# Seven block products for eight in the down-projection, with its sums of y made in the up phase

## The chip, the core and the metric

One core of a Trainium2 chip runs the whole layer in one launch. The time is device time of the launch in microseconds (us). TensorE (PE) multiplies, VectorE (DVE) and ScalarE (ACT) do elementwise work and empty PSUM, GpSimd (POOL) and the SyncE queue (SP) issue the transfers. Each engine takes its instructions in the order in which they stand in its queue; an instruction that waits holds up all that stand behind it on that engine.

## What is computed

The layer is a streaming encoder step over 1072 tokens (16 meta tokens, 1024 prompt frames, 32 sample frames). The part that the change touches is the feed-forward:

```
h = rmsnorm(x, g)
u = h @ w_up                                  # 1024 -> 2 x 2816
gate, up = u[..., :D_FF], u[..., D_FF:]
gate_ext = concatenate([gate_past, gate], axis=1)
y = silu(depthwise_causal_conv(gate_ext, dw_w, dw_b)) * up
return x + y @ w_down                          # 2816 -> 1024
```

All of it is float32. The kernel makes each float32 product from three matmuls: an operand is split into a high half (a rounded copy, made by ACT) and a low half (operand minus high half, made by DVE), and high x high, high x low and low x high are added up in PSUM.

## The kernel before

Features lie on the 128 partitions, tokens along the free axis. The 2816 hidden features are 22 tiles of 128 (f = 0 to 21), the 1024 model features are 8 tiles (k, or m on the output side).

**Up phase.** Tiles 0 and 1 are computed plainly. For tiles 2 to 21 the 2 x 2 block product (gate and up rows by two halves of the model features, times two token blocks) is made with 7 block products for 8 (`up_strassen`). The tokens are two halves p = 0 and p = 1 of two blocks of 266 or 264 tokens each (`PNS`), so a tile takes 7 products x 2 halves x 12 matmuls = 168 matmuls. The products run in the order `SEQ_ = (1, 5, 6, 2, 7, 3, 4)`, p = 0 and p = 1 in turn. Products 1, 6, 7, 4 of one half add into one PSUM bank, 5 and 3 into a second, 2 has a third; after each product the bank is copied out by ACT or added to a row by DVE, and the next product of that bank can only start after that. The moving operands (forms) of the products lie split in memory: 1 to 4 in `BH`/`BL`, 5 to 7 in `THI`/`TLO` (`th`, `tl`). The weights' forms of the next tile (sums of the weight blocks, split) are made by ACT and DVE during the present tile (`w_forms`). When the gate rows are done, `gate_done` runs the convolution and the swish over 1058 tokens, `y_done` multiplies with the up rows and stores y of the tile in DRAM (`yd`). Rows of even tiles (`rows1`) and odd tiles (`rows0`) lie in the memory of X, in `gx0` and in `rbt` (`rb`).

**Down phase.** It runs in three chunks of 8, 8 and 6 tiles (`CHUNKS`). Chunks 0 and 1 take, for each of 8 output tiles, three token blocks of 384, 352 and 320 tokens with 8 x 3 matmuls each (`d_mm`, by lines 238 to 240). Output tile m of chunk 0 is copied into X, chunk 1 adds to it. The residual (`xd`) is added by accumulating transfers that POOL issues after each second output tile of chunk 0. The weights come one output tile ahead (`d_load`). The split y of a chunk lies where the operands of the up phase lay: `y_load` brings a tile of y (528 KB) from DRAM to a staging row and `hilo` splits it (ACT the high half, DVE the low half). Chunk 0 takes four staging rows and `rbt` during tile 21; later tiles use two rows, `gx0` and `rbt`, in turn. The last chunk of 6 tiles is run together with the final norm, in an order written out by hand.

**Order.** TensorE's order is that of the code up to the end of the down phase. The order on the other engines there is set by a scheduler, which also puts SP's and POOL's transfers in a row. In the part that is written by hand at the end DVE and ACT are in the code's order too.

Of the kernel before, what the change touches and what calls it, by code (L numbers as in the profile page):

```python
# [10 lines left out]
F32 = mybir.dt.float32  # L11
# [81 lines left out]
CHUNKS = ((0, 8), (8, 16), (16, 22))  # L93
# [62 lines left out]
def body(nc, tc, cp, wp, xp, dp, io):  # L156
# [920 lines left out]
    yd = dp.tile([NF, P, T], F32, tag="yd", name="yd")  # L1077

# [48 lines left out]
    with tc.tile_pool(name="psB", bufs=1, space=PSUM, reuse_waits="tile") as pf:  # L1127
# [33 lines left out]
        def w_forms(f):  # L1161
            w = ups[f] = Up()
            g, u, s = raws3
            nc.sync.dma_start(g, up_src(f, 0))
            nc.sync.dma_start(u, up_src(f, 1))
# [3 lines left out]
            A, B = slice(0, 512), slice(512, 1024)  # L1169
# [15 lines left out]
            free.extend((hg, lg, h12, l12, a22, h34, l34))  # L1185
# [6 lines left out]
        def moving(q, p, j):  # L1192
            n, a = PNS[p], PAT[p] - H0
            b = a + n
            if q == 1:
                return BH[:, j, a:b], BL[:, j, a:b]
            if q == 2:
                return BH[:, 4 + j, a:b], BL[:, 4 + j, a:b]
            if q == 3:
                return BH[:, 4 + j, b:b + n], BL[:, 4 + j, b:b + n]  # L1200
            if q == 4:
                return BH[:, j, b:b + n], BL[:, j, b:b + n]
            i = {5: 0, 6: 1, 7: 2}[q]
# [66 lines left out]
        def y_done(f):  # L1270
            _, Tm, Y = rows_of(f)
            nc.vector.tensor_tensor(out=Y[:, NMETA:NPR], in0=Y[:, NMETA:NPR], in1=Tm[:, NMETA:NPR], op=ALU.mult)
            nc.vector.tensor_tensor(out=Y[:, NPR:T], in0=Y[:, NPR:T], in1=Tm[:, GS:GOW], op=ALU.mult)
            nc.sync.dma_start(yd[f][:, NMETA:T], Y[:, NMETA:T])

        def evac(f, p, what, ps):
            G, _, Y = rows_of(f)
            n, a0 = PNS[p], PAT[p]
            b0 = a0 + n
            ya, yb = Y[:, a0:a0 + n], Y[:, b0:b0 + n]  # L1280
            ga = G[:, g_at(a0):g_at(a0) + n]
            gb = [(lo_, hi_, G[:, o:o + hi_ - lo_]) for lo_, hi_, o in g_pieces(b0, n)]
            add = nc.vector.tensor_tensor
            if what == 1:
                nc.scalar.copy(ga, ps)
            elif what == 2:
                add(out=ga, in0=ga, in1=ps, op=ALU.add)
            elif what == 5:
                nc.scalar.copy(yb, ps)
            elif what == 6:  # L1290
                for lo_, hi_, z in gb:
                    nc.scalar.copy(z, ps[:, lo_:hi_])
            elif what == 7:
                add(out=yb, in0=yb, in1=ps, op=ALU.add)
            elif what == 3:
                for lo_, hi_, z in gb:
                    add(out=z, in0=z, in1=ps[:, lo_:hi_], op=ALU.add)
            else:
                nc.scalar.copy(ya, ps)

        BANK = {1: 0, 6: 0, 7: 0, 4: 0, 5: 1, 3: 1, 2: 2}
        SEQ_ = (1, 5, 6, 2, 7, 3, 4)
        FIRST = (1, 5, 2)

        def up_strassen(f, steps):
            gate_start(f)
            banks = {}
            for q, p in steps:
                k = p, BANK[q]
                if q in FIRST:  # L1310
                    banks[k] = mmt()[:, :PNS[p]]
                product(banks[k], q, p, f, q in FIRST)
                evac(f, p, q, banks[k])
                if (q, p) == (3, 1) and f < NF - 1:
                    gate_done(f)
                yield
# [33 lines left out]
        for i in range(4):  # L1350
            group(0, 1, i // 2, i % 2)
            if i == 0:
# [6 lines left out]
        for i, (u, p, c) in enumerate(((0, 1, 0), (0, 1, 1), (1, 1, 0), (1, 1, 1), (0, 0, 0), (0, 0, 1), (1, 0, 0), (1, 0, 1))):  # L1359
            group(1, u, p, c)  # L1360
            if i == 3:
# [25 lines left out]
        trow = [trow[i] for i in (0, 3, 1, 4, 2, 5)]  # L1387
        sr = rows(sl, 4)
        yrow = trow + [(sr[0], sr[1]), (sr[2], sr[3])] + list(zip(rows(BH, KD), rows(BL, KD))) + trow
        first = [xf[1][:, 0:ny], xf[1][:, ny:2 * ny], xf[2][:, 0:ny], xf[2][:, ny:2 * ny], rbt[:, 0:ny]]  # L1390
        first += first[:3]
        later = [gx0[:, 0:ny], rbt[:, 0:ny]]

        def y_load(f):
            raw = first[f] if f < CHUNKS[0][1] else later[f % 2]
            nc.sync.dma_start(raw, yd[f][:, NMETA:T])
            hilo(*yrow[f], raw)

        bhf, blf = flat(BH), flat(BL)
        dring = [(plain[3], plain[0]), (plain[2], plain[1])]  # L1400
        slw = [sl[:, i * 1024:i * 1024 + 1024] for i in range(4)]
# [215 lines left out]
```

## Time and profile before

| | us |
|---|---|
| median of 3 runs (1090.02 to 1090.47) | 1090.44 |
| the profiled execution | 1091.2 |
| its span in the trace | 1089.4 |
| TensorE busy | 1062.2 |
| VectorE busy | 777.3 |
| ScalarE busy | 471.9 |
| up phase from tile 2 on | 406.4 to 818.5 |
| chunks 0 and 1 of the down phase | 818.5 to 1004.0 |
| last chunk, final norm, stores | 1004.0 to 1089.4 |

The page of the profile gives the busy time of each engine and its share of the span. A busy TensorE only says that matmuls are in flight; how fast they go is read from how many start in a stretch. The timeline lists instructions with start, duration and, in brackets, the idle time before one and what ended it. An SP row with a q is the issue of a transfer, not its landing.

### The profile page before, as it was taken

What the parts mean: (1) busy time and instruction counts of PE and PEld (TensorE: products, weight loads), DVE (VectorE), ACT (ScalarE), POOL (GpSimd) and SP (SyncE); (2) the same over time, 40 slices, a digit from 0 to 9 for tenths busy, and PEclk for the clock granted to TensorE, in tenths of its full rate; (3) what the DMA queues carried; (4) which work ended last, traced back from release to release, by engine and by line L of the source; (5) the groups of instructions that cost most, each with busy time, mean ns of one, the idle gap of its engine ahead of it and who ended that gap; (6) DMA issues with size and microseconds to landing.
All of it is one profiled execution on the core that took longest, in us unless ns stands there. A gap on an engine that the chain in (4) does not pass through costs nothing.

```text
span 1089.4 us, 18949 instructions
## 1 busy us (share of the span) xinstructions
PE 1062.2 (98%) x7549; PEld 1035.2 (95%) x7549; DVE 777.3 (71%) x1355; ACT 471.9 (43%) x1009; POOL 144.9 (13%) x189
## 2 busy tenths in 40 slices
PE   8999999989999899999999999999999999999996
PEld 7999997758999899999999999999999999999996
DVE  7799999999877788778778778778777203222344
ACT  8532227996766854334334334334354214011321
POOL 1111000012435120000000001001001111000232
PEclk9999999999999999999999999999999999999998
DMA  7344331125853211321221221221267846222013
GB/s 264 81 109 100 83 95 40 39 56 82 161 147 110 66 60 60 101 77 60 99 79 59 99 79 60 97 79 60 79 237 200 193 85 159 58 63 59 15 58 102
DMA packets 48288, 103.77 MB, mean 95 GB/s; under 512 B 10048, under 2 KB 27704, under 8 KB 48200
## 3 DMA queue, kind: packets, MB, share of 16 engines
q1 hardware_dynamic: 38376, 84.46, 23.9%
q0 software_dynamic: 9536, 17.89, 9.9%
q8 instruction: 59, 0.97, 0.4%
q10 hardware_dynamic: 288, 0.22, 0.1%
q14 instruction: 29, 0.24, 0.1%
HBM read 72.41 MB, written 21.02 MB: 86 GB/s over the span
## 4 chain that ended last, share of the span: by engine, by line
PE 63%; DVE 3%; ACT 2%; issue 1%; POOL 0%; POOLq 0%; DVEq 0%; ACTq 0%
PE mm L1211 38%; PE mm L240 8%; PE mm L238 8%; PE mm L239 8%; ACT hraw L1231 1%; DVE tl L1143 1%; ACT bh L273 0%; ACT th L1142 0%; PE R L262 0%; DVE x L1485 0%; POOL rb L270 0%; ACT acc L269 0%; DVE traw L1233 0%; DVE wlo L1143 0%; DVE x L1264 0%
## 5 line engine op out<-in xcount | busy, mean ns | idle before, releaser
L364 DVE SCALAR_TENSOR_TENSOR acc<-glu,prm,acc 128x1090 f32<-128x1090 f32 (+3 forms) x180 | 168.1, 968 | 0.4
L1211 PE MATMUL mm<-bh,sl 128*128 128x266 f32 (+1 forms) x544 | 117.5, 285 | 0.0
L238 PE MATMUL mm<-hi,whi 128*128 128x352 f32 (+3 forms) x312 | 104.8, 336 | 0.0
L239 PE MATMUL mm<-lo,whi 128*128 128x352 f32 (+3 forms) x312 | 102.2, 328 | 1.6 <-DVE lo L274 1.5
L240 PE MATMUL mm<-hi,wlo 128*128 128x352 f32 (+3 forms) x312 | 101.7, 326 | 0.0
L1211 PEld LDWEIGHTS mm<-bh,sl 128*128 128x128 f32 x544 | 90.7, 189 | 0.0
L1211 PE MATMUL mm<-th,sl 128*128 128x264 f32 (+1 forms) x384 | 90.2, 285 | 0.0
L1211 PE MATMUL mm<-bl,sl 128*128 128x266 f32 (+1 forms) x296 | 84.5, 285 | 0.0
L1211 PE MATMUL mm<-bh,whi 128*128 128x266 f32 (+1 forms) x320 | 80.9, 285 | 0.0
L238 PE MATMUL mm<-bh,whi 128*128 128x266 f32 (+4 forms) x224 | 68.2, 304 | 0.0
L240 PE MATMUL mm<-bh,wlo 128*128 128x266 f32 (+4 forms) x224 | 67.9, 303 | 0.1
L239 PE MATMUL mm<-bl,whi 128*128 128x266 f32 (+4 forms) x224 | 67.9, 303 | 0.0
L1211 PEld LDWEIGHTS mm<-th,sl 128*128 128x128 f32 x384 | 66.2, 188 | 0.0
L1211 PE MATMUL mm<-th,wlo 128*128 128x266 f32 (+1 forms) x240 | 65.4, 285 | 0.0
L239 PEld LDWEIGHTS mm<-lo,whi 128*128 128x128 f32 x312 | 59.2, 190 | 3.3 <-DVE lo L274 3.0
L238 PEld LDWEIGHTS mm<-hi,whi 128*128 128x128 f32 x312 | 59.1, 189 | 1.3 <-DVE acc L364 0.6
L240 PEld LDWEIGHTS mm<-hi,wlo 128*128 128x128 f32 x312 | 59.0, 189 | 0.0
L1211 PEld LDWEIGHTS mm<-bh,whi 128*128 128x128 f32 x320 | 57.1, 189 | 0.0
L1211 PEld LDWEIGHTS mm<-bl,sl 128*128 128x128 f32 x296 | 55.8, 188 | 0.0
L1211 PE MATMUL mm<-bh,wlo 128*128 128x266 f32 (+1 forms) x208 | 51.7, 285 | 0.0
L1211 PE MATMUL mm<-th,rawr 128*128 128x266 f32 (+1 forms) x208 | 49.1, 285 | 0.0
L1211 PE MATMUL mm<-bh,rawr 128*128 128x266 f32 (+1 forms) x208 | 49.0, 285 | 0.0
(374 smaller groups left out, 3250.0 us busy)
## 6 DMA issues: line engine op xcount, KB each, us to landing
x<-wup SPq DMA_DIRECT2D x40, 512.0 KB, 4.0
wlo<-raw POOLq DMA_DIRECT2D x16, 512.0 KB, 4.5
raw<-wdn SPq DMA_DIRECT2D x16, 512.0 KB, 6.7
yd<-x SPq DMA_DIRECT2D x12, 528.0 KB, 2.9
raw<-win SPq DMA_DIRECT2D x12, 512.0 KB, 3.5
yd<-rb SPq DMA_DIRECT2D x10, 528.0 KB, 3.0
rb<-yd SPq DMA_DIRECT2D x8, 528.0 KB, 4.1
x<-yd SPq DMA_DIRECT2D x7, 528.0 KB, 5.4
```

The costliest lines, as they stand in the source:

```text
L238: nc.tensor.matmul(ps, whi(k), xhi(k), start=first and i == 0, stop=False)
L239: nc.tensor.matmul(ps, whi(k), xlo(k), start=False, stop=False)
L240: nc.tensor.matmul(ps, wlo(k), xhi(k), start=False, stop=last and i == n - 1)
L364: nc.vector.scalar_tensor_tensor(out=a, in0=e[:, a0 + k:a1 + k], scalar=pcol("cw", p * CW + k), in1=a, op0=ALU.mult, op1=ALU.add)
L1143: nc.vector.tensor_tensor(out=lo, in0=raw, in1=hi.bitcast(F32), op=ALU.subtract)
L1211: nc.tensor.matmul(ps, w[:, j, :], x, start=first and j + i == 0, stop=j == 3 and i == 2, skip_group_check=True)
L1231: nc.scalar.activation(h[:, 2 * i * n + lo_:2 * i * n + hi_], src, AF.Copy, scale=pcol("g2", k))
```

## The change

Tiles 2 to 17 (16 of 22) of the down-projection are also multiplied with 7 block products for 8. They are two chunks c = 0 and 1 of 8 tiles; within a chunk even tiles are one half of the inner features and odd tiles the other (`FORD` orders the weights so). A step is (c, mp): two output tiles, 7 products x 2 token halves x 12 matmuls on 264 tokens (`DN`); there are 8 steps. `strassen` now serves the up phase and the steps, and `w_forms` makes the weight forms of a step during the step before it. Tiles 0, 1 and 18 to 21 are the last chunk, plain as before.

The moving forms need sums of y of an even and an odd tile. `y_done` makes them in the up phase: after an even tile one subtraction and two splits (forms 1 and 5, stored split in `yh`), after an odd tile three subtractions (forms 6, 7, 4; stored whole in `yq`, with 2 and 3). `f_load` brings a form back once the product that used its place is through: 1 and 5 by two transfers that POOL issues, straight to their place; the ten others (5 forms x 2 halves) through staging rows and `hilo`. The stages are `rows1[0]`, `rows1[1]` and `rbt` in the first chunk (the first only twice), `rbt` and `rbg` in the second. So that a place is free for as long as possible, tile 21 and step (0,0) run all of p = 1 first and then p = 0 (`apart`); the others run p = 0 and p = 1 in turn. The third part of the norm of token block 2 and tile 0's `gate_done` are moved two plain groups later, and the order in which weight buffers are used again is another one.

```diff
+DN = 264
+FORD = (*range(2, 10, 2), *range(3, 10, 2), *range(10, 18, 2), *range(11, 18, 2), 0, 1, 18, 19, 20, 21)
...
+    yq = dp.tile([2, P, 7, 2, 4, DN], F32, tag="yq", name="yq")
+    yh = dp.tile([2, P, 2, 2, 2, 4, DN], F32, tag="yh", name="yh")
...
-            free.extend((hg, lg, h12, l12, a22, h34, l34))
+            used = (h12, l12, hg, lg, h34, l34, a22)
+            free.extend(z for z in used if key != ("d", 0, 0) or not any(z is r for r in rawr))
...
         def y_done(f):
...
+            if f % 2 == 0:
+                b11, b12 = halves_of(Y)
+                t1 = form_row(Tm)
+                tt_(out=t1, in0=b12, in1=b11, op=ALU.subtract)
+                for j, z, hi, lo in ((0, b11, form_row(G), form_row(G, 2 * DN)), (1, t1, form_row(Tm, 2 * DN), b11)):
+                    hilo(hi.bitcast(F32R), lo.bitcast(F32R), z)
+                    nc.sync.dma_start(yh[c, :, j, 0, :, i, :], hi)
+                    nc.sync.dma_start(yh[c, :, j, 1, :, i, :], lo)
+                return
+            _, Te, Ye = rows_of(f - 1)
+            b12, t1 = halves_of(Ye)[1], form_row(Te)
+            b21, b22 = halves_of(Y)
+            t2, t4, t3 = form_row(G), form_row(G, 2 * DN), form_row(Tm)
+            tt_(out=t3, in0=b22, in1=b12, op=ALU.subtract)
+            tt_(out=t2, in0=b22, in1=t1, op=ALU.subtract)
+            tt_(out=t4, in0=b21, in1=t2, op=ALU.subtract)
+            for q, z in ((6, t2), (2, b21), (7, t3), (3, b22), (4, t4)):
+                put(q, z)
...
+        def strassen(key, steps, dst, ns, fresh=True):
             banks = {}
             for q, p in steps:
                 k = p, BANK[q]
                 if q in FIRST:
+                    banks[k] = mmt()[:, :ns[p]]
+                product(banks[k], q, p, key, ns[p], q in FIRST)
+                for lo_, hi_, z in dst(*OUT[q], p):
+                    if fresh and q in COPY:
+                        nc.scalar.copy(z, banks[k][:, lo_:hi_])
+                    else:
+                        nc.vector.tensor_tensor(out=z, in0=z, in1=banks[k][:, lo_:hi_], op=ALU.add)
+                yield q, p
...
-            if i == 0:
+            if i == 2:
                 next(last_rms)
                 gate_done(0)
...
+        def f_load(c, q, p):
+            if q in (1, 5):
+                for j, z in enumerate(form(q, p, DN)):
+                    nc.gpsimd.dma_start(z, yh[c, :, q // 5, j, p].bitcast(F32R))
+                return
+            raw = stage(late if c else early)
+            nc.sync.dma_start(raw, yq[c, :, q - 1, p].rearrange("p a b -> p (a b)"))
+            hilo(*form(q, p, DN), raw.rearrange("p (a b) -> p a b", b=DN))
...
+        for f in range(2, NF - 1):
+            run(up_strassen(f, pairs), w_forms(f + 1, [up_src(f + 1, u) for u in range(2)], raws3))
+        run(up_strassen(NF - 1, apart), dn_forms(0, 0), lambda q, p: f_load(0, q, p),
+            (1, 3, 5, 9, 10, 11, 12))
...
+        steps = [(c, mp) for c in range(2) for mp in range(4)]
+        for i, (c, mp) in enumerate(steps):
+            hook = None
+            if mp == 3:
+                hook = last_hook if c else lambda q, p: f_load(1, q, p)
+            run(strassen(("d", c, mp), pairs if i else apart, dn_dst(mp), (DN, DN), c == 0),
+                dn_forms(*steps[i + 1]) if i < 7 else None, hook,
+                *(() if i else ((1, 3, 5, 9, 12, 12, 13),)))
+            if c == 0:
+                for b, (t0, n) in enumerate(YB):
+                    nc.gpsimd.dma_start(X[b][:, 2 * mp:2 * mp + 2, t0 - OB[b][0]:], xd[:, 2 * mp:2 * mp + 2, t0 - H0:t0 - H0 + n],
+                                        accum_op=ALU.add)
```

The first of the places where the order on an engine matters is DVE from tile 21's gate on. `x_2250`, `x_2251`, `x_2252` are the three blocks of X and the rows kept in them, `gx` is the odd tiles' gate row, `th`/`tl` with the higher number belong to p = 1. Before:

```order
L1261 TENSOR_SCALAR x_2250<-gx_3620,prm 128x1058
L1264 SCALAR_TENSOR_TENSOR x_2250<-gx_3620,prm,x_2250 128x1058 x2
L1143 TENSOR_TENSOR bl<-rb,bh 128x1056
L1268 TENSOR_TENSOR x_2250<-x_2250,rbg 128x1058
L1272 TENSOR_TENSOR x_2250<-x_2250 128x1024
L1273 TENSOR_TENSOR x_2250<-x_2250 128x32
```

Now, at the same gate, which falls into step (0,0):

```order
L1261 SCALAR_TENSOR_TENSOR x_2250<-gx_3622,prm,x_2250 128x1058 x2
L1178 TENSOR_TENSOR whi<-x_2251,wlo 128x1024
L1174 TENSOR_TENSOR gx_3622<-x_2251 128x512
L1336 TENSOR_TENSOR x_2251<-x_2251,mm 128x176
L1336 TENSOR_TENSOR x_2252<-x_2252,mm 128x88
L1265 TENSOR_TENSOR x_2250<-x_2250,rbg 128x1058
L1175 TENSOR_TENSOR gx_3622<-gx_3622,x_2251 128x512
L1176 TENSOR_TENSOR x_2251<-x_2251 128x512
L1336 TENSOR_TENSOR x_2252<-x_2252,mm 128x264
L1146 TENSOR_TENSOR bl<-x_2252,bh 128x4x264
```

The last two rows are the addition after product 7 of p = 1 and the low half of form 4 of p = 1; they stand behind the gate and behind weight forms of the next step.

The second place is DVE where a chunk's moving forms are replaced by the next one's while sums are added to X (`x_2250` to `x_2252`, the three blocks). Before, in chunk 1, where the last tiles of y come in through `gx` and `rb`:

```order
L1143 TENSOR_TENSOR tl_3619<-rb,th_3617 128x1056
L1143 TENSOR_TENSOR wlo<-raw,whi 128x1024
L1143 TENSOR_TENSOR tl_3618<-gx_3620,th_3616 128x1056
L1467 TENSOR_TENSOR x_2251<-x_2251,mm 128x384
L1143 TENSOR_TENSOR tl_3619<-rb,th_3617 128x1056
L1467 TENSOR_TENSOR x_2252<-x_2252,mm 128x352
```

Now, in step (1,0), where the forms of chunk 1 come in through `rb` and `rbg`:

```order
L1146 TENSOR_TENSOR tl_3620<-rb,th_3618 128x4x264
L1178 TENSOR_TENSOR whi<-raw,sl 128x1024
L1336 TENSOR_TENSOR x_2252<-x_2252,mm 128x264
L1336 TENSOR_TENSOR x_2250<-x_2250,mm 128x264
L1179 TENSOR_TENSOR raw<-raw,gx_3622 128x512
L1146 TENSOR_TENSOR sl<-gx_3622,sl 128x1024
L1336 TENSOR_TENSOR x_2251<-x_2251,mm 128x176
L1336 TENSOR_TENSOR x_2252<-x_2252,mm 128x88
L1146 TENSOR_TENSOR tl_3621<-rbg,th_3619 128x1056
```

The first and the last row are the low halves of form 7 of p = 0 and of p = 1. The fourth row is the addition after product 2 of p = 0 and the seventh and eighth are that of p = 1, with two steps of the weight forms of (1,1) between them; the low half of form 7 of p = 1 now stands behind all of these, where before one addition stood between two splits.

## Rows read from the trace of the kernel before

**Rows 1.** The page, engines: busy us, share of the span, instructions.

```profile
PE 1062.2 (98%) x7549; PEld 1035.2 (95%) x7549; DVE 777.3 (71%) x1355; ACT 471.9 (43%) x1009; POOL 144.9 (13%) x189
```

**Rows 2.** Busy time by stretch: length, engines (instructions), PEclk, DMA share, GB/s.

```profile
406.40:818.50 412.10, 412.10 (x3362) 412.10 (x3361) 325.62 (x458) 161.34 (x306) 27.14 (x57) 1.00 0.26 88
818.50:1004.00 185.50, 185.48 (x1154) 185.16 (x1153) 59.79 (x65) 44.36 (x59) 17.14 (x15) 1.00 0.46 116
866.00:912.00 46.00, 46.00 (x288) 46.00 (x287) 7.33 (x6) 10.93 (x18) 7.10 (x6) 1.00 0.50 92
1004.00:1075.00 71.00, 71.00 (x448) 70.99 (x447) 26.67 (x74) 18.90 (x49) 20.41 (x21) 1.00 0.15 46
```

**Rows 3.** Waits of TensorE, 320 to 410: us in total, times, longest.

```profile
PE R L262 <- ACT diag L259: 3.0, 1, 3.0
```

**Rows 4.** Busy time by stretch behind that wait, columns as in rows 2.

```profile
371.20:374.40 3.20, 3.20 (x14) 3.20 (x15) 2.21 (x5) 3.20 (x8) 0.19 (x1) 0.50 0.14 19
376.40:380.00 3.60, 3.60 (x33) 3.60 (x32) 3.56 (x7) 2.79 (x8) 0.45 (x2) 1.00 0.33 80
```

**Rows 5.** Timelines of DVE, then PE, at tile 1's second weights: start, us, instruction.

```profile
387.40 1.22 DVE L1143 TENSOR_TENSOR wlo<-raw,whi 128x1024 fp32r<-128x1024 f32 x1
...
388.68 0.39 PE L240 MATMUL mm<-bh,wlo 128*128 128x264 f32 x1
```

**Rows 6.** Timeline of DVE at tile 21's gate and the splits beside it.

```profile
818.23 1.25 DVE L1258 TENSOR_TENSOR gx<-gx,rbg 128x1060 f32<-128x1060 f32 x1
819.40 1.25 DVE L1143 TENSOR_TENSOR tl<-rb,th 128x1056 fp32r<-128x1056 f32 x1
820.57 1.22 DVE L1143 TENSOR_TENSOR wlo<-raw,whi 128x1024 fp32r<-128x1024 f32 x1
821.71 0.82 DVE L1261 TENSOR_SCALAR x<-gx,prm 128x1058 f32<-128x1058 f32 x1
822.56 2.68 DVE L1264 SCALAR_TENSOR_TENSOR x<-gx,prm,x 128x1058 f32<-128x1058 f32 x2
827.57 1.25 DVE L1268 TENSOR_TENSOR x<-x,rbg 128x1058 f32<-128x1058 f32 x1
828.86 1.23 DVE L1272 TENSOR_TENSOR x<-x 128x1024 f32<-128x1024 f32 x1
```

**Rows 7.** Groups of DVE and ACT by shape, up phase: count, busy, mean ns.

```profile
L1143 DVE TENSOR_TENSOR sl<-x,sl 128x512 fp32r<-128x512 f32 x24 | 16.5, 687 | 4.5 <-ACT x L1267 4.5
L1294 DVE TENSOR_TENSOR x<-x,mm 128x266 f32<-128x266 f32 x10 | 4.3, 426 | 0.0
L1142 ACT CAST sl<-x 128x512 fp32r<-128x512 f32 x24 | 15.0, 626 | 17.2 <-PE mm L1211 17.2
```

**Rows 8.** Timeline of SP: issues into the staging row gx.

```profile
825.32 0.32 SPq L1396 DMA_DIRECT2D gx<-yd  x1
...
831.52 0.32 SPq L1396 DMA_DIRECT2D gx<-yd  x1
...
837.64 0.32 SPq L1396 DMA_DIRECT2D gx<-yd  x1
...
844.10 0.32 SPq L1396 DMA_DIRECT2D gx<-yd  x1
```

**Rows 9.** Timeline of ACT: high halves from that row, and what ended the wait.

```profile
829.13 1.08 ACT L1142 CAST bh<-gx 128x1056 fp32r<-128x1056 f32 x1 [1.43 <-DMA gx<-yd]
835.24 1.07 ACT L1142 CAST bh<-gx 128x1056 fp32r<-128x1056 f32 x1 [2.46 <-DMA gx<-yd]
...
851.20 1.07 ACT L1142 CAST bh<-gx 128x1056 fp32r<-128x1056 f32 x1 [1.12 <-DMA gx<-yd]
```

**Rows 10.** The page, transfers: count, KB each, median us from issue to landing.

```profile
raw<-wdn SPq DMA_DIRECT2D x16, 512.0 KB, 6.7
```

**Rows 11.** Busy time by stretch at loads alone, then beside accumulating transfers, columns as in rows 2.

```profile
812.00:814.00 2.00, 2.00 (x18) 2.00 (x17) 0.72 (x2) 1.33 (x2) 0.00 (x0) 1.00 1.04 418
...
840.00:844.00 4.00, 4.00 (x27) 4.00 (x26) 2.44 (x3) 2.98 (x5) 1.18 (x1) 1.00 1.06 197
```

More of the change, by code (lines that the diff above doesn't have):

```diff
@@ L1301, in body @@
[L1301 to L1306, printed above, removed]
+            G, Tm, Y = rows_of(f)
+            tt_ = nc.vector.tensor_tensor
+            tt_(out=Y[:, NMETA:NPR], in0=Y[:, NMETA:NPR], in1=Tm[:, NMETA:NPR], op=ALU.mult)
+            tt_(out=Y[:, NPR:T], in0=Y[:, NPR:T], in1=Tm[:, GS:GOW], op=ALU.mult)
+            if not 2 <= f < 18:
+                nc.sync.dma_start(yd[f][:, NMETA:T], Y[:, NMETA:T])
+                return
@@ L1366, in body @@
                 free += [sl[:, i * 1024:i * 1024 + 1024] for i in range(4)]
-                free += [wp.tile([P, 1024], F32R, tag="raw", name="rawr") for _ in range(2)]
-                free += plain
-                forms = w_forms(2)
+                rawr = [wp.tile([P, 1024], F32R, tag="raw", name="rawr") for _ in range(2)]
+                free += rawr + plain
+                forms = w_forms(2, [up_src(2, u) for u in range(2)], raws3)
                 next(forms)
@@ L1386, in body, with stage, y_load @@
         trow = [(h, l) for p in range(2) for h, l in zip(rows(THI[p], 3), rows(TLO[p], 3))]
[L1387 to L1397, printed above, removed]
+        yrow = [trow[i] for i in (0, 3, 1, 4, 2, 5)]
+        yf = (0, 1, 18, 19, 20, 21)
+        early = [rows1[0][:, 0:ny], rows1[1][:, 0:ny], rbt[:, 0:ny]]
+        early += early[:1] + 3 * early[1:]
+        late = [rbt[:, 0:ny], rbg[:, 0:ny]]
+        nst = [-1]
+        def stage(st):
+            nst[0] += 1
+            return st[nst[0] % len(st)]
+        def f_load(c, q, p):
+            if q in (1, 5):
+                for j, z in enumerate(form(q, p, DN)):
+                    nc.gpsimd.dma_start(z, yh[c, :, q // 5, j, p].bitcast(F32R))
+                return
+            raw = stage(late if c else early)
+            nc.sync.dma_start(raw, yq[c, :, q - 1, p].rearrange("p a b -> p (a b)"))
+            hilo(*form(q, p, DN), raw.rearrange("p (a b) -> p a b", b=DN))
+        def y_load(i):
+            raw = stage(late)
+            nc.sync.dma_start(raw, yd[yf[i]][:, NMETA:T])
+            hilo(*yrow[i], raw)
         bhf, blf = flat(BH), flat(BL)
-        dring = [(plain[3], plain[0]), (plain[2], plain[1])]
-        slw = [sl[:, i * 1024:i * 1024 + 1024] for i in range(4)]
-        last_w = {1: slw[:2], 2: slw[2:]}
-        last_w.update({i + 3: (bhf[:, i * 1024:i * 1024 + 1024], blf[:, i * 1024:i * 1024 + 1024]) for i in range(5)})
         nscr = [0]
@@ L1447, in body, with run @@
+        def run(gen, forms, hook=None, at=(1, 3, 5, 7, 9, 11, 13)):
+            for i, (q, p) in enumerate(gen):
+                for _ in range(at.count(i) if forms else 0):
+                    next(forms, None)
+                if hook:
+                    hook(q, p)
             for _ in forms or ():
                 pass
+        for f in range(2, NF - 1):
+            run(up_strassen(f, pairs), w_forms(f + 1, [up_src(f + 1, u) for u in range(2)], raws3))
+        run(up_strassen(NF - 1, apart), dn_forms(0, 0), lambda q, p: f_load(0, q, p),
+            (1, 3, 5, 9, 10, 11, 12))
```

186 lines of the change are left out of this document (77 added, 109 removed).

## The prediction, made before the changed kernel was run

> **What bounds the kernel now.** I read the page's engines first [rows 1]: TensorE is busy for 98% of the span, and VectorE, next, for 71%. So time goes only with fewer or narrower matmuls, or comes only with a wait of TensorE. The busy times by stretch [rows 2] show that this holds stage by stage: in the up phase and in the chunks TensorE is busy throughout, at a granted clock of 1.00, while VectorE works 325.6 of 412.1 us in the up phase and 59.8 of 185.5 us in the chunks. The list of TensorE's waits [rows 3] has one of 3.0 us, for ACT's R of the norm, about 371 us after the start. Behind it the granted clock is 0.50 (1.2 GHz) for 3.2 us, in which 14 matmuls start, and 1.00 again later, 33 in 3.6 us [rows 4]. At the later pace the 14 would take 14 x 0.109 = 1.5 us, so such a wait costs up to 1.7 us beside its own 3.0; I take 1.5. The question is therefore not whether the matmuls saved are worth their time, but whether the new operands come in time.
>
> **Matmuls removed.** A plain chunk step is 288 matmuls in 46.00 us [rows 2], 0.1597 us each for 352 columns on average; chunks 0 and 1 have 1152, 184.0 us. Now they have 8 steps x 7 products x 2 halves x 12 = 1344 of 264 columns. The up phase gives their price: 3360 in 412.1 us [rows 2], 0.1227 us at 265 columns on average, 0.1222 at 264. That is 164.2 us: **-19.8 us** if no operand is late. A product is then 1.47 us, a step or an up-phase tile 20.5.
>
> **Sums in the up phase.** The added work of a pair of tiles is six operations of VectorE on 528 columns (one subtraction and two low halves after the even tile, three subtractions after the odd one), two casts of ACT, and nine more transfers of SP. An operation with 512 columns takes 0.69 us, a cast 0.63 [rows 7]. VectorE works 325.6/20 = 16.3 us of a tile's 20.6; with 3 x 0.69 = 2.1 it has 18.4. What hides them is that slack of 2.2 us, and the weight forms of the next tile, which are needed only a tile later. 0; if the cover is gone, the additions behind them are late (a rival, below).
>
> **The early stage.** R and tile 0's gate stand two groups later, so the wait of [rows 3] goes, with its clock: at most -4.5. But VectorE is the engine behind it, and tile 1's second weights are split at 387.40 and the first matmul with their low half starts at 388.68 [rows 5], as soon as the split is done: that split, behind the same work of VectorE, is late next. I take 0, between -4.5 and +1.5 (a wait moved to where it costs a clock drop of its own).
>
> **Refill 1, tile 21 and step (0,0).** Let T be the start of tile 21. Product 4 of p = 1 of (0,0) can start at T + 20.5 + 6 x 1.47 = T + 29.3. Its low half is the last of the DVE rows shown in the change. The queue ahead of it starts with the addition after product 3 of p = 0 of tile 21, at T + 19.5; then, by the steps from one start to the next in [rows 6] and the durations of [rows 7], the gate's first multiplication and three low halves (forms 7 and 3, and a weight), 4 x 1.17; TENSOR_SCALAR 0.85; the two STT 2.68; three weight-form operations, 3 x 0.69; the additions 0.7 and 0.43; the multiplication at L1265 1.25; and form 4 itself 1.17. Together 13.8: T + 33.3, a wait of 4.0. Before, this gate held up nothing, since no form stood behind it.
> From there two staging rows set the pace (`x_2252` and `rb`). One cycle of a row is the load, the cast and the low half. Before, the row `gx` was filled at 825.32, 831.52 and 837.64 [rows 8], so 6.2 us; the cast starts 3.81 after the issue [rows 9]. Form 2 of p = 0 takes the row of form 4 of p = 1: T + 33.3 + 6.2 = T + 39.5. Form 7 of p = 0 stands behind it in VectorE's queue, with three weight splits, an addition and itself between: 0.69 + 1.17 + 0.69 + 0.43 + 0.69 + 1.17 = 4.8, T + 44.3. Form 4 of p = 0 has the row of form 7: T + 50.5, and its product ends at T + 52.0 in place of T + 41.0: **+11.0**. Lower end +8.5: the weight splits ahead of form 7 (2.5) are done in the wait before. The upper end is contention, below.
>
> **Refill 2, step (0,3) and (1,0).** Let S be the start of (0,3). In (1,0) product 2 of p = 0 ends at S + 30.8. The second place of the change shows what follows on VectorE: its addition 0.43, two weight-form steps 0.69 and 1.17, the addition for p = 1 0.7, form 7 of p = 1 1.17: S + 35.0, needed at S + 33.7. Forms 3 and 4 of p = 1 take the same row `rbg` in turn: S + 35.0 + 2 x 6.2 = S + 47.4, and product 4 ends at S + 48.9 in place of S + 41.0: **+7.9** (6 where the two weight steps are done before).
>
> **Contention.** Beside these loads stand POOL's: eight transfers of forms 1 and 5 per refill, and accumulating ones of the residual. Alone, loads keep the 16 DMA engines at a share of 1.04 and 418 GB/s; beside accumulating transfers the same share moves 197 GB/s [rows 11]. There the issue at 844.10 [rows 8] led to a cast only at 851.20 [rows 9], 7.1 us instead of 3.8, and weight loads have a median of 6.7 [rows 10]. That would lengthen a cycle by 3.3. Of the four cycles on the path I take 0.6 in this state: **+2.0** (0 to 4).
> The Trainium skill, "DMA: Bandwidth & Descriptors" (Anatomy of one DMA), gives a fixed cost of about 2 us and a rate of 436 GB/s; for 528 KB that is an estimate of 3.2 us. The trace's 3.8 is above it and 7.1 far above; by the page's figure a cycle would be 0.6 us shorter and the two refills together about 2.4 us less.
>
> **Clock.** Each refill ends with a gap of some 3 us in front of its last product. By [rows 4] the clock falls behind it: 2 x 1.5 = **+3.0** (0 to 3). Drops at gaps before that cost nothing, as the rows pace TensorE there.
> The Trainium skill, "TensorE: Matmul & The Clock Gate" (Part 1: The HAM clock gate), says that throttled is the default and activity releases it, between 1.2 and 2.4 GHz alone. The granted 0.50 and 1.00 of [rows 4] agree; the page's reading that the ramp is a small matter in a typical span would put this term near 0.
>
> **The rest.** Steps (0,1) to (0,3) and (1,1) to (1,3) need weight forms alone, made a step ahead; VectorE had 59.8 of 185.5 us in the chunks and has room. 0 (to +2). The last chunk and the norm, 85.4 us, have the same matmuls; their y comes in during (1,3). 0.
>
> **Sum.** 1089.4 - 19.8 + 0 + 11.0 + 7.9 + 2.0 + 3.0 = 1093.5 of span. The profiled execution is 1.8 above its span and 0.8 above the median, so the median is span + 1.0: **1094.5 us**, 0.4% slower. A measurement of this kernel tells some 0.2% (2.2 us) from no change.
>
> **Rivals.**
> - Faster: the refills are hidden. A form's place falls free a whole step before it is needed, and the loads run while TensorE has other products. If VectorE takes splits before the gate's long operations (I have anchored its queue at one addition; earlier waits would shift it), both waits shrink. It decides by the cycle: a half step of 10.3 us uses five staged forms, so two rows keep up without any head start at 2 x 10.3/5 = 4.1 us. With none of 23.9 us left 1070.6; with half 1082.5. Against it: the cycle of 6.2 in [rows 8] had no rival load in the first place.
> The Trainium skill, "Trainium Kernel Development and Optimization" (Best Practices), has it that double buffering overlaps DMA and compute; by that rule the two rows suffice. In [rows 9] the cast waits 1.43 and 2.46 for the load in spite of two rows, so here it speaks for less than half.
> - About the same: the mechanism holds, but landings stay at 3.8 and the clock costs nothing: 1089.5, and with the lower ends of the refills down to 1085.
> - Much slower: the sums also hold up TensorE in the up phase. The additions after product 7 stand behind the even tile's subtraction and two splits (3 x 0.69 = 2.1); product 4 needs the bank one product (1.47) later. From 0.7 us without another cover, TensorE waits; with a clock drop 0.7 + 0.8 = 1.5 per pair x 8 = 12: 1106.5.
> - The change doesn't save what it says, as 264 columns cost more beside transfers: in the worst transfers of [rows 11] TensorE starts 27 matmuls in 4.0 us, 0.148 each, no slower than the 0.1597 of a chunk step. I give it next to nothing.
>
> **Chances.** The forecast (1092.6 to 1100) 0.36; about the same 0.25, of which 0.03 lies below 1088.3; refills half hidden 0.17, fully hidden 0.10; up phase held up 0.08; anything slower in other places 0.04. That makes faster 0.30, same 0.22, slower 0.48. Leaving out fully hidden and the up phase, the range is 1079 to 1101; the forecast's own range is 1092.6 to 1100.
>
> **What would show it.** Right: step (0,0) takes some 31 us and (1,0) some 28 against 20.5 in the other steps, with TensorE's waits at product 4 of p = 1 and at products 7 and 4 of p = 0 in (0,0), and at 7, 3 and 4 of p = 1 in (1,0), ended by DVE low halves; the up phase stays 412 us. Wrong: steps (0,0) and (1,0) near 20.5 (the queue or the cycle was mis-sized), an up phase longer by over 5 us, or a wait near 371 to 389 us that is gone without a successor.

## The result, and the profile after

| | before | after |
|---|---|---|
| median (5 runs each) | 1090.47 | 1095.29 |
| lowest to highest | 1090.02 to 1091.31 | 1093.53 to 1098.15 |
| span of the profiled execution | 1089.4 | 1093.5 |

The ratio is 1.0048 (95% interval 1.0027 to 1.0068): the kernel became half a per cent slower, 4.8 us. The engines of the page of after, to be held against [rows 1]:

```profile
PE 1050.1 (96%) x7741; PEld 1019.4 (93%) x7741; DVE 860.3 (79%) x1559; ACT 499.8 (46%) x1077; POOL 168.2 (15%) x205
```

TensorE is busy for 12 us less, and the span is 4 us longer: it waits now. The table of stretches says where. It is cut at tile 2, tile 21, steps (0,0), (0,1), (1,0), (1,1) and the last chunk, each taken from the first matmul of product 5 less the products ahead of it; columns as in [rows 2].

```profile
406.13:798.10 391.97, 391.51 (x3194) 391.30 (x3193) 331.62 (x485) 154.92 (x302) 40.14 (x55) 1.00 0.33 106
798.10:822.75 24.65, 22.53 (x170) 22.10 (x169) 17.88 (x25) 9.73 (x17) 7.40 (x10) 0.93 1.02 294
822.75:853.10 30.35, 23.02 (x171) 21.17 (x171) 24.46 (x33) 15.11 (x25) 4.26 (x5) 1.00 0.68 214
853.10:914.65 61.55, 61.55 (x507) 61.55 (x506) 31.55 (x57) 23.87 (x53) 13.92 (x15) 1.00 0.73 170
914.65:946.95 32.30, 25.50 (x170) 23.86 (x170) 20.10 (x35) 11.52 (x14) 3.63 (x3) 0.89 0.79 233
946.95:1008.40 61.45, 61.45 (x505) 61.45 (x504) 39.10 (x88) 17.05 (x20) 0.00 (x0) 1.00 0.30 95
1008.40:1093.50 85.10, 75.30 (x480) 74.92 (x478) 37.26 (x102) 21.76 (x55) 21.88 (x23) 0.96 0.22 67
```

The same cuts of before, for the up phase and its last tile:

```profile
406.21:797.80 391.59, 391.59 (x3196) 391.59 (x3195) 308.64 (x438) 147.18 (x285) 27.14 (x57) 1.00 0.24 80
797.80:818.50 20.70, 20.70 (x171) 20.70 (x170) 17.17 (x21) 14.16 (x21) 0.00 (x0) 1.00 0.65 234
```

Six of the eight steps take 20.5 us (61.55/3 and 61.45/3), with TensorE busy throughout. Tiles 2 to 20 take what they took, though VectorE has 23 us more work there. The losses stand in three places: tile 21 (24.65 for 20.70), step (0,0) (30.35) and step (1,0) (32.30). The waits of TensorE from tile 21 on (us in total, times, longest) name the splits of forms, VectorE's low halves above all, one copy of ACT, and two additions of VectorE:

```profile
PE mm L1208 <- DVE tl L1146: 5.0, 2, 3.2
PE mm L1208 <- DVE bl L1146: 4.2, 5, 1.2
PE mm L1208 <- ACT bh L1145: 2.2, 2, 1.3
PE mm L1208 <- ACT gx L1334: 1.9, 1, 1.9
PE mm L1208 <- DVE x L1336: 1.4, 2, 1.2
```

As a sum: up to the end of tile 20 +0.3 us, tile 21 +4.0, chunks 0 and 1 without waits -21.3 (185.5 in [rows 2] against 8 x 20.5 = 164.2), (0,0) +9.8, (1,0) +11.8, the last chunk -0.3: +4.3, and the spans differ by 4.1.

**Tile 21.** Timelines of POOL, SP, ACT and TensorE (start, us, instruction, and in brackets the idle time before and what ended it):

```profile
800.10 0.85 POOL L1429 DMA_DIRECT2D bl<-yh  x1
...
802.29 0.56 POOL L1429 DMA_DIRECT2D th<-yh  x1
804.73 0.33 SPq L1432 DMA_DIRECT2D x<-yq  x1
811.91 1.07 ACT L1145 CAST th<-x 128x1056 fp32r<-128x1056 f32 x1 [2.97 <-DMA x<-yq]
812.89 0.37 ACT L1334 COPY gx<-mm 128x266 f32<-128x266 f32 x1
813.31 0.39 PE L1208 MATMUL mm<-th,sl 128*128 128x266 f32 x1 [1.90 <-ACT gx L1334]
```

The first staged form is issued at 804.73, behind POOL's four direct loads, and lands 7.2 us later. Its cast waits for it on ACT, and the copy after product 1 of p = 0 stands behind the cast, though TensorE went on to product 5 some three us earlier. Until that copy is made, product 6 can't use the bank. Behind the wait the granted clock falls:

```profile
813.30:817.00 3.70, 3.69 (x17) 3.69 (x18) 2.75 (x3) 2.15 (x6) 0.00 (x0) 0.55 1.32 355
```

**Step (0,0).** VectorE's timeline: the gate's first multiplication, the low halves of form 4 of p = 1 and of forms 2, 7 and 4 of p = 0; and SP's issues of the last three of these forms, into `x` (`x_2252`), `rb`, `rb`.

```profile
821.63 1.26 DVE L1255 TENSOR_TENSOR gx<-gx,rbg 128x1060 f32<-128x1060 f32 x1
...
833.34 1.25 DVE L1146 TENSOR_TENSOR bl<-x,bh 128x1056 fp32r<-128x1056 f32 x1
...
839.22 1.26 DVE L1146 TENSOR_TENSOR bl<-x,bh 128x1056 fp32r<-128x1056 f32 x1 [1.28 <-ACT bh L1145]
...
844.27 1.25 DVE L1146 TENSOR_TENSOR tl<-rb,th 128x1056 fp32r<-128x1056 f32 x1
...
850.28 1.26 DVE L1146 TENSOR_TENSOR bl<-rb,bh 128x1056 fp32r<-128x1056 f32 x1 [0.39 <-ACT bh L1145]
```

```profile
834.62 0.32 SPq L1432 DMA_DIRECT2D x<-yq  x1
...
837.97 0.32 SPq L1432 DMA_DIRECT2D rb<-yq  x1
...
845.55 0.32 SPq L1432 DMA_DIRECT2D rb<-yq  x1
```

Each issue follows the end of the low half that frees its row at once (833.34 + 1.25 to 834.62; 844.27 + 1.25 to 845.55). From one low half to the next of the same row it is 5.9 us (form 4 to form 2, in `x`) and 6.0 us (form 7 to form 4, in `rb`); from form 6 to form 7 in `rb` it is 7.6 us, as form 7 stands behind weight splits on VectorE.

### The profile page after: what moved, and what is told of

It is laid out like the page before. It is cut to its first block, busy times and chain, and to the rows that moved or that the text cites. A ratio compares the mean times of both kernels' runs of the same rounds, so it can differ in the third digit from the quotient of the medians.

```text
span 1093.5 us, 19782 instructions
## 1 busy us (share of the span) xinstructions
PE 1050.1 (96%) x7741; PEld 1019.4 (93%) x7741; DVE 860.3 (79%) x1559; ACT 499.8 (46%) x1077; POOL 168.2 (15%) x205
## 4 chain that ended last, share of the span: by engine, by line
PE 55%; DVE 6%; DMA 3%; ACT 3%; issue 2%; POOL 0%; POOLq 0%; DVEq 0%; ACTq 0%; SPq 0%
PE mm L1208 46%; PE mm L241 3%; PE mm L239 3%; PE mm L240 3%; DMA x<-yq 1%; DVE tl L1146 1%; DMA raw<-wdn 1%; DVE bl L1146 1%; ACT hraw L1228 1%; DMA x<-wdn 0%; ACT th L1145 0%; DMA rbg<-yq 0%; DVE x L1336 0%; DVE sl L1146 0%; DMA rb<-yq 0%
## 5 line engine op out<-in xcount | busy, mean ns | idle before, releaser
L1208 PE MATMUL mm<-bh,sl 128*128 128x264 f32 (+1 forms) x752 | 163.0, 286 | 1.8 <-ACT bh L1145 1.3
L1208 PE MATMUL mm<-bl,sl 128*128 128x264 f32 (+1 forms) x376 | 108.2, 288 | 0.9 <-DVE bl L1146 0.9
L1208 PE MATMUL mm<-bh,whi 128*128 128x264 f32 (+1 forms) x384 | 102.2, 288 | 2.2 <-DVE x L1336 1.2
L1208 PE MATMUL mm<-bh,wlo 128*128 128x264 f32 (+1 forms) x384 | 101.6, 287 | 0.2 <-DVE x L1336 0.2
L1208 PE MATMUL mm<-tl,sl 128*128 128x264 f32 (+1 forms) x296 | 85.1, 288 | 3.3 <-DVE tl L1146 3.2
L1336 DVE TENSOR_TENSOR x<-x,mm 128x264 f32<-128x264 f32 (+6 forms) x190 | 61.3, 352 | 31.8 <-PE mm L1208 31.1
L1208 PE MATMUL mm<-th,wlo 128*128 128x264 f32 (+1 forms) x272 | 77.7, 285 | 0.0
L1208 PE MATMUL mm<-th,whi 128*128 128x264 f32 (+1 forms) x272 | 77.6, 285 | 0.0
L1208 PEld LDWEIGHTS mm<-bh,wlo 128*128 128x128 f32 x384 | 70.6, 191 | 0.4 <-DVE x L1336 0.4
L1208 PE MATMUL mm<-bh,rawr 128*128 128x264 f32 (+1 forms) x272 | 61.5, 286 | 0.0
```

The lines of the kernel that those rows point to most:

```text
L1208: nc.tensor.matmul(ps, w[:, j, :], x[:, j, :], start=first and j + i == 0, stop=j == 3 and i == 2, skip_group_check=True)
L1336: nc.vector.tensor_tensor(out=z, in0=z, in1=banks[k][:, lo_:hi_], op=ALU.add)
```

## Experiments

All times are medians on the chip beside runs of the kernel before on the same chip (1090.1 to 1090.7). "The changed kernel" is the one above, 1095.3.

### Without the loads

```diff
         def f_load(c, q, p):
+            return
```

> All loads of moving forms in the down phase are left out (f_load returns at once), so chunks 0 and 1 multiply what lies in the places of the forms; sums, stores, weight forms, copies and additions stay. Theory: the time over an unhindered kernel sits in tile 21 (24.6 us for 20.6) and in steps (0,0) and (1,0) (30.4 and 32.3 us for 20.5), and all of it comes from forms that are late or from what stands behind their casts: 4.0 + 9.9 + 11.8 = 25.7 us less, about 1070 us, and all three at 20.5 to 20.6 us. Rival: VectorE's and ACT's other work there (tile 21's gate, the weight forms of the next step, additions) or the weight loads set these steps: then half or more stays, 1080 us or above.

Measured: 1072.69 us, a ratio of 0.9838 (0.9819 to 0.9858). Tile 21, (0,0) and (1,0):

```profile
797.19:817.74 20.55, 20.55 (x170) 20.55 (x169) 14.98 (x23) 6.72 (x14) 1.72 (x2) 1.00 0.23 70
817.74:839.78 22.04, 20.82 (x170) 20.61 (x169) 15.49 (x25) 7.92 (x18) 3.21 (x5) 1.00 0.38 105
901.30:921.80 20.50, 20.50 (x170) 20.50 (x169) 12.09 (x28) 4.41 (x7) 3.00 (x3) 1.00 0.48 106
```

Of 25.6 us lost in the three places 24.2 go; 1.5 stay in (0,0), where the addition after a product stands behind tile 21's gate on VectorE. The kernel still makes and stores every sum of y in the up phase and is 18 us faster than before (20 us by the spans of the profiled executions): the sums cost TensorE nothing, and what the change saves is there. What is lost is lost in bringing the forms back. The run takes out the transfers and the splits together, so it doesn't tell which of the two is late.

### The early stage put back

```diff
-            if i == 2:
+            if i == 0:
                 next(last_rms)
                 gate_done(0)
```

> Undoes one part of the change: the third part of the norm and tile 0's gate stand again two plain groups earlier. Theory: that part only moved a wait. TensorE's wait of about 3 us at 371 us comes back with its clock drop, its waits of 1.7 and 2.1 us at 384 and 387 us go, and the up phase starts at 406 us as in both kernels: 1094 to 1096.5, no different from the changed kernel. Rival: the part brings 3 to 4 us that something else in the changed kernel eats, and without it the kernel takes 1098 to 1100.

Measured: 1095.09 us, as the changed kernel. The waits of TensorE from 360 to 406 us in the changed kernel, and the one in this kernel:

```profile
PE mm L241 <- DVE wlo L1146: 2.1, 1, 2.1
PE mm L239 <- ACT whi L1145: 1.7, 1, 1.7
```

```profile
PE R L263 <- ACT diag L260: 3.0, 1, 3.0
```

The part moved a wait from the norm ([rows 3]) to tile 1's second weights.

This run shows one thing more. The edit doesn't touch tile 21, and TensorE waits there for the same copy and as long as in the changed kernel, but the granted clock behind the wait stays at 1.00, and the tile takes 23.2 us for 24.65 (TensorE's timeline, then the stretch behind the wait, columns as in [rows 2]):

```profile
812.90 0.39 PE L1208 MATMUL mm<-th,sl 128*128 128x266 f32 x1 [1.90 <-ACT gx L1334]
812.90:816.60 3.70, 3.70 (x30) 3.70 (x31) 3.29 (x4) 3.15 (x6) 0.00 (x0) 1.00 1.40 374
```

So the fall of the clock is worth some 1.5 us there, and it came in some of the profiled executions only. In those whose edits leave tile 21 and (0,0) alone (this one, the changed kernel, and three further down in which only the residual's transfers, POOL's order or refill 2 are edited) tile 21 takes 22.4 to 24.7 us, and the two stretches together 53.4 to 55.0 us. What an edit gains there is read from the two together.

### Tile 21's copy by VectorE

```diff
+                    if key == NF - 1 and (q, p) == (1, 0):
+                        nc.vector.tensor_copy(z, banks[k][:, lo_:hi_])
-                    if fresh and q in COPY:
+                    elif fresh and q in COPY:
```

> One copy of tile 21, that after product 1 of p = 0, is made by VectorE and not by ACT, where it stands behind the cast of form 6 of p = 1, which waits 3.0 us for its load. Theory: TensorE's wait of 1.9 us at 813 us and the clock drop behind it go, tile 21 falls from 24.6 to about 21 us, and the kernel is 3 to 4 us faster than the changed kernel: 1091.5 to 1092.5. Rival: the loads are late in any case, and what tile 21 gains step (0,0) gives back, since its forms come no sooner: 1094 to 1096.

Measured: 1093.71 us (1091.68 to 1094.62), between the two. Tile 21 takes 22.1 us, 2.5 less, (0,0) 30.3 as before, (1,0) 33.1. The wait for that copy is gone; one of 1.3 us for an addition of VectorE stands in its place. Tile 21 and (0,0) together take 52.4 us, so of the 2.5 us only 1.0 are clear of what tile 21 does without the edit, and the times of the two kernels overlap (1093.53 to 1098.15 us for the changed one).

### A third staging row in refill 1

```diff
+        r0, r1, r2 = early
+        early = [r0, r1, r2, r0, r1, r2, rbg[:, 0:ny], r1, r2, rbg[:, 0:ny]]
...
+        for q in (2, 7, 3, 4):
+            f_load(0, q, 0)
```

The four loads are called after tile 21's gate, since `rbg` holds R until then.

> Refill 1 gets a third staging row for its last four forms: rbg, free once tile 21's gate is through. Theory: two rows in turn set the pace; forms 2, 7, 3, 4 of p = 0 then take rbg, a row, rb, rbg, the last of them is split some 4 to 5 us sooner, step (0,0) takes 25.5 to 26.5 us instead of 30.4, and the kernel 1090 to 1091.5. Rival: the transfers share 16 DMA engines that are busy anyway (share 0.68 in this step), so that a third load in flight only slows the other two: under 1 us, 1094 to 1096.

Measured: 1090.51 us, 4.8 less than the changed kernel. Step (0,0) takes 27.5 us for 30.35. Tile 21, which this edit doesn't touch, came out at 22.6, so not all of the 4.8 us are the third row's: the two together take 50.1 us, 3.3 to 4.9 us less than without the edit.

### Loads in halves

```diff
+            for a in (0, 2):
+                r = raw[:, a * DN:(a + 2) * DN]
+                nc.sync.dma_start(r, yq[c, :, q - 1, p, a:a + 2].rearrange("p a b -> p (a b)"))
+                hilo(hi[:, a:a + 2], lo[:, a:a + 2], r.rearrange("p (a b) -> p a b", b=DN))
```

> Each staged form is loaded and split in two halves of 264 KB, each in one half of its staging row, so that load, cast and low half of the halves overlap; no memory is added. Theory: the cycle of a row (6 to 7 us for 528 KB, of which the load is about 4 and the splits 2.3) sets the pace of both refills; a half cycles in 4 to 5 us and four are in flight, so a form takes 2.0 to 2.5 us instead of 3.1 and the refills lose a third to a half of their 21.7 us: 1084 to 1089. Rival: bandwidth and the queues of ACT and VectorE are the limit, more and smaller transfers win nothing: 1094 to 1097.

Measured: 1087.46 us, a ratio to before of 0.9971 (0.9958 to 0.9984). (0,0) 26.2 us, (1,0) 27.2: 9.2 of the 21.6 us, as the theory of the rows has it. Tile 21 and (0,0) together take 49.3 us. No byte less is moved. In the wait list of this kernel a new item leads, POOL's direct loads of form 5 in (1,0):

```profile
PE mm L1208 <- DMA th<-yh: 2.6, 1, 2.6
```

### Three edits together

The copy by VectorE, the third row and the halves, as in the diffs above.

> Three edits at once: tile 21's one copy by VectorE, rbg as third row for the last four forms of refill 1, and loads in halves. Theory: three different waits, so the gains add where they lie in different steps: tile 21 21.5 to 22.5 us, (0,0) 24 to 25.5, (1,0) about 27, the kernel 1081 to 1084.5. Rival: with halves the transfers are the limit, and a third row wins nothing more: 1085.5 to 1088, as with halves alone.

Measured: 1085.79 us: the rival's number. (0,0) 25.3 and (1,0) 26.5 us fall into or near what was expected; tile 21 doesn't (24.0). The copy made by VectorE now stands behind other splits there, so this edit gave nothing beside the others. Tile 21 and (0,0) together take 49.3 us, as with the halves alone: there the third row wins nothing more, as the rival has it.

### Without the residual's transfers near refill 2

```diff
-            if c == 0:
+            if c == 0 and mp < 2:
                 for b, (t0, n) in enumerate(YB):
                     nc.gpsimd.dma_start(X[b][...], xd[...], accum_op=ALU.add)
```

> The residual's accumulating transfers for the output tiles of steps (0,2) and (0,3) are left out; nothing else is. Theory: they take bandwidth from refill 2 (157 to 200 GB/s at 896 to 904 us with the engines always busy, 350 to 420 after that), so forms come sooner without them: (1,0) takes 28 to 30 us instead of 32.3, the kernel 1091 to 1093.5. Rival: rows and the queues of VectorE alone set (1,0): 31.5 us or more, 1094.5 to 1096.

Measured: 1085.84 us, a far larger gain than either theory had. (1,0) takes 22.99 us. A stretch of 6 us at POOL's direct loads, in the changed kernel and in this one (the last two columns are the DMA share and GB/s):

```profile
897.00:903.00 6.00, 6.00 (x52) 6.00 (x51) 2.00 (x4) 3.47 (x10) 5.33 (x8) 1.00 1.19 212
```

```profile
896.00:902.00 6.00, 6.00 (x52) 6.00 (x51) 2.23 (x4) 3.33 (x10) 4.22 (x7) 1.00 1.30 313
```

With the accumulating transfers the DMA engines are nearly as busy (1.19 against 1.30) and move 212 GB/s, without them 313.

### The residual later

Written later in the code, with POOL's queue in the order of the code, and beside the three edits:

```diff
-            if c == 0:
+            for mp in {0: (0,), 1: (1,), 4: (2,), 5: (3,)}.get(i, ()):
```

> The three edits, and the residual of steps (0,2) and (0,3) is added only after (1,0) and (1,1), for which POOL's queue is put in the order of the code too. Theory: refill 2 gets the bandwidth of the transfers moved away, (1,0) falls to 23 to 25 us, the kernel 1077 to 1082. Rival: the loads of the forms fill the engines by themselves, or the residual's transfers hold up the additions of (1,2) and (1,3) later: as the three edits alone, 1081 to 1085.

Measured: 1084.96 us, as the rival had it, because the edit did not do what it says: POOL issued the first three of these transfers at 895.6 us, right behind the direct loads, as nothing made them wait, and (1,0) took 27.1 us. So a wait was made, in the changed kernel without the three edits, with POOL's queue again in the order of the code: a copy of one column of the last sum of a step, which POOL can only make when that step is through.

```diff
+            if i in (4, 5):
+                nc.gpsimd.tensor_copy(held[:, i - 4:i - 3], X[2][:, 2 * mp + 1, 0:1])
+            for r in {0: (0,), 1: (1,), 4: (2,), 5: (3,)}.get(i, ()):
...
```

> The changed kernel with one edit: the residual of steps (0,2) and (0,3) is added after refill 2. POOL's queue is in the order of the code, and one-column copies of the last sums of (1,0) and of (1,1) stand ahead of the transfers and hold them back. Theory: these transfers set the length of (1,0) beside the loads; it falls to 23 us as with the transfers left out, and nothing takes their place: 1085 to 1087.5. Rival: moved, they hold up additions or loads in (1,1) to (1,3): these steps take more than 20.6 us, 1089 to 1095.

Measured: 1087.15 us, a ratio to before of 0.9968 (0.9958 to 0.9977). POOL issues the transfers at 939.12 and 960.28, (1,0) takes 24.05 us, and the steps behind it 20.5 and 20.6. Nothing took their place.

### What the transfers did in (1,0)

Holding the transfers back also moved instructions: the low half of form 7 of p = 1, which in the changed kernel stands behind the addition after product 2, now stands ahead of it. VectorE's timeline of the changed kernel, from the step of the next weights that waits for its load to that low half:

```profile
921.58 0.69 DVE L1174 TENSOR_TENSOR gx<-raw 128x512 f32<-128x512 f32 x1 [3.30 <-DMA raw<-wdn]
...
925.59 1.26 DVE L1146 TENSOR_TENSOR tl<-rb,th 128x1056 fp32r<-128x1056 f32 x1 [0.96 <-ACT th L1145]
...
930.72 1.25 DVE L1146 TENSOR_TENSOR tl<-rbg,th 128x1056 fp32r<-128x1056 f32 x1
```

And with the residual held back, where the step begins 0.8 us earlier:

```profile
917.54 0.69 DVE L1174 TENSOR_TENSOR gx<-raw 128x512 f32<-128x512 f32 x1 [1.62 <-DMA raw<-wdn]
...
920.51 1.26 DVE L1146 TENSOR_TENSOR tl<-rb,th 128x1056 fp32r<-128x1056 f32 x1 [0.27 <-ACT th L1145]
921.69 0.42 DVE L1336 TENSOR_TENSOR x<-x,mm 128x264 f32<-128x264 f32 x1
922.02 1.25 DVE L1146 TENSOR_TENSOR tl<-rbg,th 128x1056 fp32r<-128x1056 f32 x1
```

Counted from the start of the step, the weight load lets VectorE go on 3.2 us later in the changed kernel, form 7 of p = 0 is split 4.3 us later, and that of p = 1 7.9 us later. So by the traces at most 4.3 us are the transfers' doing: 3.2 through the weight load, which holds up ACT and VectorE ahead of the splits, and 1.1 on ACT, where the cast of form 7 of p = 0 stands behind a weight cast in the changed kernel and ahead of it here. The other 3.6 us are the order's on VectorE. The next run was to tell them apart on the chip:

```diff
+                if behind:
+                    nc.vector.tensor_tensor(**low.pop())
+                    behind.__exit__(None, None, None)
...
+            if (c, q, p) == (1, 7, 1):
+                nc.scalar.copy(hi, z)
+                low.append(dict(out=lo, in0=z, in1=hi.bitcast(F32), op=ALU.subtract))
...
```

> The kernel with the residual held back, and one operation moved: the low half of form 7 of p = 1 in refill 2 stands on VectorE again behind the additions after product 2 of p = 1 (and, as the queue then falls out, after product 7 of p = 0) of step (1,0), about where the changed kernel has it; holding the residual back had also moved it ahead of them. Theory: its place in VectorE's queue sets when rbg is filled again, so (1,0) grows from 24.0 to 29 to 31.5 us without any residual transfer near it, and the kernel takes 1092 to 1095. Rival: the transfers alone had lengthened (1,0); it stays at 24 to 25.5 us, 1086.5 to 1088.5.

Measured: 1093.27 us, (1,0) 29.3 us, the numbers of the theory, but not by its way. The operation now reads `rbg` after the row was filled again (its low half is of another form's data), so it waits for the last load and starts only at 933.44, while the row is filled as early as with the residual held back:

```profile
PE mm L1208 <- DVE tl L1341: 7.0, 1, 7.0
```

It shows that one low half split 11 us later costs (1,0) 5.3 us with no residual near. What the shift of 3.6 us costs in the changed kernel it doesn't show: how much of (1,0) is the transfers' and how much the order's stays open, and the traces alone speak to it.

### All that helped

The residual held back, loads in halves, and the third row, as in the diffs above:

> The residual held back, loads in halves, and rbg as third row of refill 1. Theory: three waits of different kinds; with the transfers away refill 2 is set by the rows, and halves shorten that: (1,0) 20.5 to 22 us, (0,0) 24.5 to 26, tile 21 22.5 to 24, the kernel 1076 to 1081. Rival: the loads of the forms fill the engines also without the residual, (1,0) stays at 23 and the kernel at 1081 to 1084.

Measured: 1078.64 us (1077.70 to 1080.18), ratio to before 0.9896 (0.9879 to 0.9912): 1.0% faster than before and 16.7 us faster than the changed kernel. Tile 21, (0,0) and (1,0):

```profile
798.08:822.02 23.94, 21.18 (x171) 20.73 (x170) 18.51 (x28) 10.72 (x21) 8.11 (x11) 1.00 1.00 287
822.02:846.77 24.75, 21.56 (x170) 20.74 (x169) 23.56 (x39) 15.13 (x31) 1.29 (x3) 1.00 0.73 236
908.44:929.03 20.59, 20.59 (x171) 20.59 (x170) 19.09 (x41) 11.53 (x19) 0.00 (x0) 1.00 0.65 208
```

Refill 2 is hidden altogether: (1,0) takes 20.59 us, with TensorE busy throughout. Tile 21 and (0,0) together take 48.7 us, 0.6 less than with the halves alone. With the high half of the first form made by VectorE as well:

```diff
...
+                if (c, q, p) == (0, 6, 1):
+                    nc.vector.tensor_copy(hi[:, a:a + 2], r)
+                    nc.vector.tensor_tensor(out=lo[:, a:a + 2], in0=r, in1=hi[:, a:a + 2].bitcast(F32), op=ALU.subtract)
...
```

> As the one before, and the high half of form 6 of p = 1 in refill 1 is made by VectorE, so that no copy of ACT stands behind a cast that waits for the first load. Theory: tile 21 falls to 21 to 22.5 us, 1 to 2 us less in all. Rival: the same wait comes back behind VectorE's queue, as with the copy made by VectorE: no difference.

Measured: 1079.82 us. The wait came back, as the rival has it: in tile 21 (25.9 us) an addition of VectorE now stands behind a low half whose load is late.

```profile
820.72 0.59 PE L1208 MATMUL mm<-bh,wlo 128*128 128x266 f32 x1 [3.40 <-DVE x L1336]
```

What tile 21 would need (fewer bytes in flight from 800 us on, or splits that stand later in both queues) was not tried.

## Why the prediction was right, and where not

Forecast 1094.5 us, measured 1095.29, slower as forecast. Step by step:

- **Matmuls removed, -19.8.** Right, a little small: 8 steps of 20.5 us took the place of 185.5 us. I had priced the plain chunks by their undisturbed step of 46.00 us [rows 2]; the first of them took 47.5 (818.5 to 866), so 21.3 went.
- **Sums in the up phase, 0.** Right: tiles 2 to 20 took 391.97 us, and 391.59 before; without the loads the kernel with all its sums was 18 us faster than before.
- **The early stage, 0.** Right, and for the reason given: putting it back changed nothing.
- **Refill 1, +11.0.** Right by its mechanism and its steps: from the end of the addition after product 3 to the end of form 4's low half 13.8 us were worked out, and it was 13.0 (821.63 to 834.59); then a cycle of 6.2 (5.9), 4.8 behind the weight splits (5.0; the sum counts four of them where its words say three, and four there were), a cycle (6.0). Its anchor was 4.0 us late, but the step began late by the same; so +9.8. Halves (26.2 us) and the third row (27.5) bear out that the rows set the pace.
- **Refill 2, +7.9, and contention, +2.0.** The size is right, +11.8 with the clock, and the waits are the three that were named (forms 7, 3 and 4 of p = 1: 3.2, 2.2 and 1.25 us). The end of form 7's low half was worked out at 14.5 us into (1,0) and came at 17.3 (931.97), then two cycles of 7.2 and 6.3. But contention was mis-sized: I put it into the cycle of a staging row, where these two cycles hold 1.1 us of it, and its larger effect was on the load of the next weights, whose steps stand ahead of the splits on ACT and VectorE. Leaving the transfers out took 9.3 us off (1,0), holding them back 8.3. How much of that is their own doing stays open: of the 7.9 us by which form 7 of p = 1 was split later, the traces give them at most 4.3, and the rest to an order that came with them.
- **Clock, +3.0.** The price of one fall was right, the places were wrong. The same wait of tile 21 with and without a fall behind it differs by some 1.5 us, as priced. But (0,0) kept 1.00 through all its waits, and the falls came in tile 21 and in (1,0), there behind the waits for forms 7 and 3 of p = 1 and not behind the last product's:

```profile
932.00:936.00 4.00, 3.98 (x22) 3.98 (x23) 2.57 (x5) 0.62 (x1) 0.00 (x0) 0.64 0.67 171
940.00:944.00 4.00, 3.94 (x20) 3.73 (x18) 2.52 (x5) 1.07 (x1) 0.00 (x0) 0.58 0.87 239
```

  In (1,0) further waits follow each of them and take in part of the loss; how much, no run shows.
- **What was missing: tile 21, +4.0.** I looked at VectorE's queue from the gate on, and not at ACT's in tile 21, where a copy stands behind the cast of the first load. "Refill 1" named the transfers of POOL only under contention; here they stood ahead of the first load. The step that failed is the zero for the up phase's end. That the sum still came out at the measured span, 1093.5 us, is luck: tile 21 (+4.0) was made up for by the matmuls (1.5 more saved) and by the two refills with contention and clock (21.6 measured for 23.9).

The rival "the refills are hidden" would have needed other waits: the fastest version has refill 2 hidden, but with finer loads and with the residual out of the way, not by two rows alone. One argument against that rival was misread: the cycle of 6.2 us in [rows 8] did have other loads beside it (SP issued a load of weights at 832.66 and one of y into `rb` at 833.83). The estimate of 3.2 us for 528 KB by the Trainium skill, "DMA: Bandwidth & Descriptors" (Anatomy of one DMA), lay below the medians of the staged forms. That page's fit is for transfers that GpSimd issues, and these are issued by SP, beside others; the measurement decides. Issue to landing from 804 to 852 us in the changed kernel, last column:

```profile
x<-yq SPq DMA_DIRECT2D x6, 528.0 KB, 6.8
rb<-yq SPq DMA_DIRECT2D x5, 528.0 KB, 3.6
```

## What to carry to other kernels

Work that is saved on the engine that bounds shows only where its operands can come in time: look at the moment at which a set of operands is replaced, count the bytes, the staging rows and one row's whole cycle (load, cast, subtraction), and every instruction that stands ahead of the splits on their engines. A cast that waits for a transfer holds up the copies behind it, and with them TensorE's banks. Cheap remedies are smaller pieces in the same rows, and moving unrelated transfers out of that time by something that they must wait for, since their place in the code alone doesn't hold them.

## What the hardware showed that I had not expected

- Beside accumulating transfers nearly as busy DMA engines moved a third less, theirs included: 212 GB/s at a share of 1.19 against 313 at 1.30 without them (6 us at POOL's direct loads). A weight load of 512 KB let its reader on VectorE go on 8.1 us after its issue (913.44 to 921.58) against 4.9 with the residual held back (912.67 to 917.54).
- Waits of the same length had different effects on TensorE's clock. Behind the 1.90 us at 813 us the granted clock was 0.55 (near 1.2 GHz) for 3.7 us; behind the same 1.90 us in the run with the early stage put back it was 1.00, and so it was behind 1.85 us at 845.57, in a step with 7 us of waits:

```profile
843.40:847.70 4.30, 2.07 (x13) 1.66 (x13) 3.40 (x6) 1.07 (x1) 0.00 (x0) 1.00 0.54 163
```

- Five executions of the changed kernel spread over 4.6 us, those of before over 1.3. A fall of the clock that comes in some executions only, worth 1.5 us in tile 21, can be part of that; no run shows that it is all of it.
